# Hybrid S5 / gated DeltaNet / RWKV-7 block: triangular inverses from 16-blocks and masked products instead of 32-blocks

## The chip, the cores and the metric

One core of a Trainium2 chip runs the whole program in one launch. The metric is the device time of that core in microseconds, taken as the median of three runs. Engine names are those of the profile: PE is the matrix engine, PEld its weight loads, DVE the vector engine, ACT the scalar engine, POOL the general engine, and SP the engine whose queue issues every DMA of this kernel.

## What is computed

Two layers of a diffusion trunk. Each layer projects 256 context tokens and 512 latent tokens to three groups of heads, mixes them over the tokens, projects back and applies an MLP. Two of the three mixers work in chunks of 64 tokens, in both directions, and need per chunk, head and direction the inverse of a unit triangular 64 x 64 matrix. In the reference it stands as a solve:

```python
m = jnp.where(strict, jnp.einsum('bhnik,bhnjk->bhnij', kb, k) * decay, 0.0)
rhs = jnp.concatenate([v * beta[..., None], kb * jnp.exp(g)[..., None]], axis=-1)
sol = lax.linalg.triangular_solve(m + jnp.eye(C, dtype=m.dtype), rhs, left_side=True,
                                  lower=True, unit_diagonal=True)
...
def step(s, inp):
    kd_n, u_n, w_n, gl_n = inp[:4]
    v_new = u_n - jnp.einsum('bhck,bhkv->bhcv', w_n, s)
    s_next = s * jnp.exp(gl_n)[..., None, None] + jnp.einsum('bhck,bhcv->bhkv', kd_n, v_new)
```

The RWKV-7 mixer is a token-by-token scan in the reference; the kernel brings it to the same chunked form. The dense products (projections and MLP) are float32 with K = 1024 or 4096.

## The kernel before

The mixers' work is cut into 12 *pairs*, numbered 0 to 11 here: layer 0 context (pairs 0 to 2), layer 0 latents (3 to 5), layer 1 context (6 to 8), layer 1 latents (9 to 11). A pair holds one DeltaNet job and one RWKV job of two heads each. A context pair has 4 chunks, a latent pair 8. For a pair the kernel emits these steps:

- *prep* of both jobs (L1395 with `within`, L1359, and L1536): the strictly triangular matrices N. The last products of prep are L1622 and L1630 on PE; L1633 on POOL writes the last piece of N.
- *solve* (L335 to L386): the 32 x 32 diagonal blocks of N are stored to memory (L352), loaded so that every block lies on one partition (L363, L364), one half transposed by ACT (L366), inverted by substitution on DVE (L371, L373; 30 rounds of a product and a sum), transposed (L375), stored (L376 to L379) and loaded back into place (L352) together with transposes (L386).
- *prep2* (L1638): RWKV's b and k are transposed by PE (L481), copied by ACT (L1648) and parked in memory. It does not read the inverses. It frees the arena pages that held b and k.
- *post* (L1422, L1655): `level2` (L388) joins the 32-blocks to 64-blocks by two rounds of small products (L398, L404); then the inverses are applied (L1439, L1441, L1670 to L1682).
- *chain* (L1466, L1690): the recurrence over the chunks, on PE (L1488, L1502, L1511 for DeltaNet, L1708, L1722, L1732, L1733 for RWKV) and DVE (L1490, L1504, L1710, L1724) in turns.
- *readout*.

The order of emission is set by `run_jobs` (L1257): prep, solve and prep2 of pair i + 1 come ahead of post, chain and readout of pair i. Classes of priority (`CHAIN`, `LEVEL`, `READ`, `PREP`, `S5`, `DENSE`) let a scheduler take urgent work first, and it writes a fixed queue for each engine, which the engine works off in that order. Dense work (L296) and the S5 mixer (L779 to L900) are emitted in low classes and stand in the queues between the pairs' steps.

Two resources are handed out in the order of emission. PSUM banks come by tag with two buffers each: prep and prep2 use tag "p", post uses "q", the chains "gc" and "rc", dense work and S5 "d". SBUF comes from an arena of 18 pages (`s`, `scope`, `release`), so that a later tile can lie in a page that an earlier step still reads. The tile "solve" is a single buffer.

Of the kernel before, what the change touches and what calls it, by code (L numbers as in the profile page):

```python
# [12 lines left out]
OP = mybir.AluOpType  # L13
AX = mybir.AxisListType

P = 128
# [4 lines left out]
T = CT + LT  # L21
# [3 lines left out]
# tags of small shared tiles: columns, buffers  # L25
TAGS = {"s": (516, 6), "g1": (256, 3), "r1": (128, 3), "carry": (128, 6), "gup": (128, 2),
        "td": (24, 4), "tp": (24, 4), "tq": (24, 4), "tg": (24, 4), "tr": (24, 4), "t5": (8, 6), "wc": (24, 4),
        "solve": (2048, 1)}
# [12 lines left out]
for _n, _w in (("ident", 128), ("lt_f", 128), ("lt_b", 128), ("p_f", 128), ("p_b", 128),  # L41
               ("ones", 128), ("mr", 128), ("rm", 256), ("bo2", 2),
               ("sel2", 128), ("cent", 128), ("bo128", 128), ("scan", 512)):
    CONST[_n] = (_o, _w)
    _o += _w
# [19 lines left out]
class Part:  # L65
    """the context or the latents: first token, tokens, modulation's column."""
# [23 lines left out]
class Kern:  # L90
# [26 lines left out]
    def prio(self, c):  # L117
        """what is emitted inside is scheduled before the higher classes, in its own order."""
# [33 lines left out]
    def set_rounded(self, count):  # L152
        """makes count of the pages hold float32r."""
# [13 lines left out]
    def own(self, count, late, pieces):  # L167
        """lets what the pieces emit take its tiles from count pages of its own; late: jobs that they outlast."""
# [15 lines left out]
    def s(self, w, p=P, keep=None, kind=None):  # L184
# [12 lines left out]
                # early free, not beside tiles of another life, not across quarters and halves  # L197
# [36 lines left out]
    def load_layer(self, l):  # L234
# [4 lines left out]
        # derived columns  # L239
# [25 lines left out]
    def weight(self, src, eng):  # L265
        """the parts of 128 rows of up to 512 values; eng: the engines that take turns at the low one."""
# [9 lines left out]
    def rows(self, src, eng):  # L276
        """by row tile the parts of 4 x 128 rows of a block of 128 columns."""
# [12 lines left out]
    def product(self, ps, w, acts, first=True, last=True, fresh=False):  # L290
        """ps += sum over k of w[k].T @ act[k]; fresh: the low parts of acts come last."""
# [6 lines left out]
    def dense(self, src, acts, n, eng, fresh=False):  # L298
        """out^T[128 cols, tokens] for one block of 128 columns, in psum."""
# [6 lines left out]
    def rows_rstd(self, ps, n, scale, eps, tag):  # L306
        """(ps * scale + eps) ** -0.5 on a small token-major tile."""
# [7 lines left out]
    def bcast(self, r, w, sel, nt, tag, rt):  # L315
        """r [128 tokens, w per tile] back to feature-major, in psum; rt: scratch."""
# [18 lines left out]
    def solve(self, probs, nc_):  # L335
        """probs: pairs of blk, ytt. blk(h): [128, step, direction, 64] whose rows of half h hold strictly
        triangular blocks N on their diagonal; the inverses of I - N replace them. ytt takes the transposes
        of every first one."""
# [5 lines left out]

        def blocks(dram, store):
# [1574 lines left out]
```

## Time and profile before

| | |
|---|---|
| median of 3 runs | 3077.45 us (3076.12 to 3078.54) |
| span of the profiled execution, first to last instruction | 3056.7 us |
| PE / DVE / ACT / POOL busy | 87% / 60% / 39% / 37% of the span |
| granted PE clock, mean | 0.875 of 2.4 GHz |
| substitution on DVE (L371 and L373) | 720 instructions, 294.1 us |

The profile is of one execution; its own time is known as the span alone, and the runs' median is 20.75 us above it. A busy PE is not a PE at its peak, since records overlap and at half the clock the same work looks twice as long. Every float32 product leaves two records on PE.

### The profile page before, as it was taken

The page shows a single profiled execution, that of the slowest core. Times are in us where ns is not written, and L with a number is a line of the kernel's source. Part 1 is how long each engine was busy: PE and PEld are TensorE (multiplying, and loading weights), DVE is VectorE, ACT ScalarE, POOL GpSimd, SP SyncE. Part 2 cuts the span into 40 slices and gives each one's busy share as a digit, 9 for nine tenths or more (in the row PEclk, how much of TensorE's full clock was granted, in tenths as well). Part 3 has the DMA queues.
Part 4 walks back from the last instruction along what each step waited for, and adds up shares of the span by engine and source line. Part 5 has one row for each costly group of instructions (what it writes and reads, how often), then busy time and mean ns, then how long its engine had stood idle before and what let it go on. Part 6 is the DMA issues. An engine that isn't in the chain of part 4 may idle for free.

```text
span 3056.7 us, 54445 instructions
## 1 busy us (share of the span) xinstructions
PE 2669.4 (87%) x19956; PEld 2044.2 (67%) x19956; DVE 1833.7 (60%) x4462; ACT 1186.7 (39%) x2411; POOL 1134.5 (37%) x1274
## 2 busy tenths in 40 slices
PE   5789998865898999987899989889887889799998
PEld 1667776543566888876666768667655567477776
DVE  6654878765667756647876562647776753332223
ACT  2344445332534543445423423353334432133332
POOL 2532335424133121123446644344442522244443
PEclk9788999676787999987999999889987859699998
DMA  5345546543653543535233332255555632022222
GB/s 196 96 140 185 151 136 210 154 130 86 200 161 120 166 157 116 167 114 161 85 88 111 125 96 93 102 187 159 148 184 165 211 93 86 28 83 94 93 94 86
DMA packets 324651, 401.73 MB, mean 131 GB/s; under 512 B 142880, under 2 KB 173472, under 8 KB 324256
## 3 DMA queue, kind: packets, MB, share of 16 engines
q1 hardware_dynamic: 324384, 398.24, 41.6%
q8 instruction: 158, 2.59, 0.4%
q14 instruction: 109, 0.89, 0.1%
HBM read 300.76 MB, written 88.90 MB: 127 GB/s over the span
## 4 chain that ended last, share of the span: by engine, by line
PE 53%; DVE 19%; DMA 9%; issue 5%; ACT 4%; SPq 3%; POOL 1%; DVEq 0%; ACTq 0%; POOLq 0%
PE d L296 35%; DMA page<-dr 3%; DVE solve L371 3%; DVE solve L373 3%; PE rc L1733 2%; DVE wo L273 2%; PE rc L1732 2%; PE p L1622 1%; DVE s L472 1%; DMA dr<-page 1%; SPq L352 1%; DMA s<-s 1%; DMA wl<-in_w_dram 1%; ACT wh L272 1%; PE p L481 1%
## 5 line engine op out<-in xcount | busy, mean ns | idle before, releaser
L296 PE MATMUL d<-page,wh 128*128 128x512 f32 (+1 forms) x5024 | 1424.8, 367 | 61.0 <-DVE page L1156 15.5
L296 PEld LDWEIGHTS d<-page,wh 128*128 128x128 f32 x5024 | 919.0, 196 | 234.5 <-DVE page L1156 18.0
L296 PE MATMUL d<-page,wo 128*128 128x512 f32 (+1 forms) x2512 | 915.2, 365 | 5.5 <-DVE wo L273 4.3
L272 ACT CAST wh<-wl 128x512 fp32r<-128x512 f32 (+1 forms) x750 | 457.1, 616 | 710.2 <-PE d L296 421.0
L273 POOL TENSOR_TENSOR wo<-wl,wh 128x512 fp32r<-128x512 f32 (+1 forms) x357 | 471.8, 1325 | 672.0 <-ACT wh L272 635.8
L296 PEld LDWEIGHTS d<-page,wo 128*128 128x128 f32 x2512 | 493.4, 196 | 80.6 <-DVE wo L273 5.8
L273 DVE TENSOR_TENSOR wo<-wl,wh 128x512 fp32r<-128x512 f32 (+1 forms) x393 | 296.1, 758 | 112.6 <-ACT wh L272 104.1
L1156 DVE SCALAR_TENSOR_TENSOR page<-d,mod,page 128x512 f32<-128x512 f32 (+1 forms) x192 | 124.8, 659 | 199.6 <-PE d L296 199.1
L371 DVE TENSOR_TENSOR solve<-solve 128x30 f32<-128x30 f32 (+4 forms) x360 | 151.3, 420 | 21.6 <-issue 12.0
L1147 DVE TENSOR_TENSOR s<-s 128x512 f32<-128x512 f32 (+1 forms) x96 | 60.5, 631 | 172.1 <-ACT s L1146 172.0
L373 DVE TENSOR_TENSOR solve<-solve 128x30 f32<-128x30 f32 (+4 forms) x360 | 142.8, 397 | 7.7
L1499 POOL TENSOR_TENSOR g<-g,gates 64x128 f32<-64x128 f32 x120 | 59.5, 496 | 219.7 <-DVE g L1504 190.4
L285 DVE TENSOR_TENSOR page<-s,page 128x512 fp32r<-128x512 f32 (+1 forms) x118 | 86.6, 738 | 47.5 <-ACT page L284 47.3
L1146 ACT ACTIVATE s<-d 128x512 f32<-128x512 f32 (+1 forms) x96 | 50.6, 527 | 141.5 <-PE d L296 141.4
L472 DVE SCALAR_TENSOR_TENSOR s<-s,ncol,s 128x256 f32<-128x256 f32 (+1 forms) x132 | 96.4, 733 | 3.0
L284 ACT CAST page<-s 128x512 fp32r<-128x512 f32 (+1 forms) x118 | 64.1, 547 | 80.5 <-DVE s L1147 62.9
L926 PE MATMUL d<-wo,scp 128*2 128x512 f32 x160 | 76.3, 477 | 20.6 <-DVE wo L273 19.6
L1622 PE MATMUL p<-page,page 64*128 64x128 f32 (+1 forms) x576 | 84.7, 307 | 10.4 <-DVE page L1625 7.1
L1622 PEld LDWEIGHTS p<-page,page 64*128 64x128 f32 x576 | 73.1, 209 | 27.4 <-issue 12.8
L1733 PE MATMUL rc<-page,page 128*64 128x64 f32 x464 | 86.7, 275 | 2.8 <-DMA page<-dr 2.8
L481 PE MATMUL p<-consts,page 128*128 128x128 f32 x348 | 63.8, 309 | 25.0 <-DMA page<-dr 11.2
L1732 PE MATMUL rc<-page,r 64*64 64x64 f32 x432 | 79.2, 270 | 5.6 <-DVE r L1724 4.0
(464 smaller groups left out, 4057.7 us busy)
## 6 DMA issues: line engine op xcount, KB each, us to landing
wl<-in_w_dram SPq DMA_DIRECT2D x384, 256.0 KB, 2.6
wl<-in_mod_w_dram SPq DMA_DIRECT2D x160, 256.0 KB, 3.0
wl<-in_w_in_dram SPq DMA_DIRECT2D x142, 256.0 KB, 2.9
page<-dr SPq DMA_DIRECT2D x118, 256.0 KB, 3.3
dr<-s SPq DMA_DIRECT2D x72, 256.0 KB, 2.5
dr<-page SPq DMA_DIRECT2D x30, 512.0 KB, 4.1
dr<-page SPq DMA_DIRECT2D x55, 256.0 KB, 2.5
page<-dr SPq DMA_DIRECT2D x16, 834.0 KB, 5.2
```

The lines of the kernel that those rows point to most:

```text
L272: nc.scalar.copy(hi, st)
L273: low.tensor_tensor(lo, st, hi.bitcast(F32), OP.subtract)
L285: nc.vector.tensor_tensor(lo, src, hi.bitcast(F32), OP.subtract)
L296: nc.tensor.matmul(ps, x, y, start=(first and i == 0), stop=(last and i == len(order) - 1))
L371: nc.vector.tensor_tensor(tm, y3[:, :j, j:j + 1].to_broadcast([P, j, w]), y3[:, j:j + 1, j + 1:].to_broadcast([P, j, w]), OP.mult)
L373: nc.vector.tensor_tensor(y3[:, :j, j + 1:], y3[:, :j, j + 1:], tm, OP.add)
L472: nc.vector.scalar_tensor_tensor(acc, cp[:, j:j + n], w[:, 5 * i + j:5 * i + j + 1], acc, OP.mult, OP.add)
L481: self.nc.tensor.transpose(p[:, t * 128:(t + 1) * 128], src[:, t * 128:(t + 1) * 128], self.ident)
L1156: nc.vector.scalar_tensor_tensor(x[j], ps, mod[:, 40 + j, g:g + 1], x[j], OP.mult, OP.add)
L1622: nc.tensor.matmul(ps[:, i], flat(bk[d][hs, n0 + i]), kr[d][hs, n0 + i], start=True, stop=True)
L1732: nc.tensor.matmul(o, st[hs, d], kr[d][hs, n, 1], start=True, stop=False)
L1733: nc.tensor.matmul(o, xv[h][:, n, d], self.R[d][:, h, n], start=False, stop=True)
```

## The change

The substitution now inverts only the two 16 x 16 blocks on the diagonal of each 32-block, both in one instruction (`b2`, 14 rounds). A new step `level1` joins them to 32-blocks before the inverses go on: per job it makes two rounds of small products on PE in PSUM banks of tag "p", an ACT copy that scales by a 0/1 column (`lowhalf`), twelve DVE updates that read the products from PSUM under the same masks, and four POOL copies. The second load after the substitution now takes the transposes of both directions into the "solve" tile, which `level1` reads. Nothing else is moved in the source; all comments are removed, so line numbers from `solve` on shift (in `post` and `chain` by 39).

```diff
         "solve": (2048, 1)}
+        "solve": (2112, 1)}
...
+               ("ones", 128), ("mr", 128), ("rm", 256), ("bo2", 2), ("lowhalf", 2),
...
-        for j in range(30, 0, -1):
-            w = 31 - j
-            tm = yt[:, :j * w].rearrange("p (a b) -> p a b", a=j)
-            nc.vector.tensor_tensor(tm, y3[:, :j, j:j + 1].to_broadcast([P, j, w]),
-                                    y3[:, j:j + 1, j + 1:].to_broadcast([P, j, w]), OP.mult)
-            nc.vector.tensor_tensor(y3[:, :j, j + 1:], y3[:, :j, j + 1:], tm, OP.add)
+        b2 = w[:, :1056].rearrange("p (s x) -> p s x", s=2)[:, :, :512].rearrange("p s (a b) -> p s a b", b=32)
+        for j in range(14, 0, -1):
+            v = 15 - j
+            tm = yt[:, :2 * j * v].rearrange("p (s a b) -> p s a b", s=2, a=j)
+            nc.vector.tensor_tensor(tm, b2[:, :, :j, j:j + 1].to_broadcast([P, 2, j, v]),
+                                    b2[:, :, j:j + 1, j + 1:16].to_broadcast([P, 2, j, v]), OP.mult)
+            nc.vector.tensor_tensor(b2[:, :, :j, j + 1:16], b2[:, :, :j, j + 1:16], tm, OP.add)
...
-        blocks(dy, False)
-        dr = dt.rearrange("(j h k n d) a b -> j h k d a n b", j=len(probs), h=2, k=2, d=2)
-        for j, (_, ytt) in enumerate(probs):
-            for d in range(2):
-                for h in range(2):
-                    p0 = 64 * h + 32 * d
-                    nc.sync.dma_start(ytt[p0:p0 + 32], dr[j, h, d, d])
+        mts = [w[:, 512 * j:512 * j + 64 * nc_].rearrange("p (n d i) -> p n d i", d=2, i=32) for j in range(len(probs))]
+        for j, h, k, ps in places:
+            sb = probs[j][0][ps].rearrange("p n d i -> p (n d) i")[:, :, k * 32:k * 32 + 32]
+            nc.sync.dma_start(sb, split(dy)[j, h, k])
+            nc.sync.dma_start(mts[j][ps].rearrange("p n d i -> p (n d) i"), split(dt)[j, h, k])
+        for j, ((blk, ytt), mt) in enumerate(zip(probs, mts)):
+            self.level1(blk, mt, ytt, w[:, 1056 + 512 * j:1056 + 512 * j + 64 * nc_], nc_, "p")
+
+    def level1(self, blk, mt, ytt, qv, nc_, tag):
...
+        pv = blocks(self.ps(tag, n2), 32)
+        for n, d, p0 in every:
+            u, v = pair(slice(p0, p0 + 16), n, d, p0)
+            nc.tensor.matmul(pv[p0:p0 + 32, n, d], u, v, start=True, stop=True)
+        nc.scalar.mul(qv, pv.rearrange("p n d i -> p (n d i)"), hi)
+        qv = blocks(qv, 32)
+        po = self.ps(tag, 48 * nc_)
...
+        for n, d, p0 in every:
+            r = slice(p0, p0 + 32)
+            u, q = pair(r, n, d, p0)[0], qv[r, n, d]
+            outs = [(px[r, n, d], d == 0)] + [(pt[r, n], d == 1)] * (p0 % 64 == 32 * d)
+            for out, first in outs:
+                if first:
+                    nc.tensor.matmul(out, q, u[:, 16:], start=True, stop=True)
+                else:
+                    nc.tensor.matmul(out, u, q[:, :16], start=True, stop=True)
+        cut = ((16, hi), (0, lo))
+        for p0 in range(0, P, 32):
+            r = slice(p0, p0 + 32)
+            for d, (c, keep) in enumerate(cut):
+                x = blk[r, :, d, p0 % 64 + c:p0 % 64 + c + 16]
+                nc.vector.scalar_tensor_tensor(x, x, keep[r], px[r, :, d], OP.mult, OP.add)
...
+            nc.vector.scalar_tensor_tensor(ytt[r, :, c:c + 16], mt[r, :, d, c:c + 16], keep[r], pt[r], OP.mult, OP.add)
+            nc.gpsimd.tensor_scalar(ytt[r, :, 16 - c:32 - c], mt[r, :, d, 16 - c:32 - c], 1.0, None, OP.mult)
```

The order of the queues changes with it. The first place is PE's queue where prep of pair 11 ends and chain 10 is under way, in the kernel before. The names are: `p_` for banks of prep and prep2, `gc_` for the DeltaNet chain, `q_` for post. L1630 is the last product of prep 11, L481 is prep2 of pair 11, L1502 and L1511 are steps of chain 10, and L398 begins `level2` of pair 10.

```order
L1630 MATMUL p_24625<-page_117,page_4007 64x64
L481 MATMUL p_24745<-consts,page_109 128x128 x4
L481 MATMUL p_24751<-consts,page_109 128x128 x4
L481 MATMUL p_24759<-consts,page_115 128x128 x4
L481 MATMUL p_24765<-consts,page_115 128x128 x4
L1502 MATMUL gc_25096<-g_4050_25093,page_105 64x64 x2
L1502 MATMUL gc_25096<-g_4050_25093,page_97 64x64 x2
L481 MATMUL q_24905<-consts,page_119 128x128 x4
L481 MATMUL q_24915<-consts,page_4013 128x128 x4
L1511 MATMUL gc_25096<-page_115,g_4050_25093 64x64
L398 MATMUL q_24924<-page_97,page_111 32x32 x32
```

The same place in the changed kernel (L1669 is the former L1630, L1541 the former L1502, L403 the first round of `level1`):

```order
L1669 MATMUL p_27251<-page_117,page_4173 64x64
L1541 MATMUL gc_28048<-g_4098_28045,page_105 64x64 x2
L1541 MATMUL gc_28048<-g_4098_28045,page_97 64x64 x2
L403 MATMUL p_27339<-solve_27282,page_105 32x32 x4
L403 MATMUL p_27339<-page_105,solve_27282 32x32 x4
```

From there 320 products of `level1` (L403, L414, L416) stand in one piece, with nothing of another step between them, and behind the last of them (L520 is the former L481, L1550 the former L1511, L438 the former L398):

```order
L414 MATMUL p_27584<-solve_27282 32x16
L416 MATMUL p_27584<-solve_27282 32x16 x2
L414 MATMUL p_27584<-solve_27282 32x16
L520 MATMUL p_27697<-consts,page_109 128x128 x4
L520 MATMUL p_27703<-consts,page_109 128x128 x4
L520 MATMUL p_27711<-consts,page_115 128x128 x4
L520 MATMUL p_27717<-consts,page_115 128x128 x4
L520 MATMUL q_27857<-consts,page_119 128x128 x4
L520 MATMUL q_27867<-consts,page_4179 128x128 x4
L1550 MATMUL gc_28048<-page_115,g_4098_28045 64x64
L438 MATMUL q_27876<-page_97,page_111 32x32 x32
```

So prep2 of pair 11 and the rest of chain 10 have moved behind `level1` of pair 11.

The second place is PE's queue at the start of chain 9, in the kernel before. L481 here is prep2 of pair 10, which reads page_19841; L1488 is the first product of chain 9, which reads its W from the same page; L925, L926 and L839 are modulation and S5.

```order
L1630 MATMUL p_23519<-page_4009,page_97 64x64
L481 MATMUL p_23639<-consts,page_19841 128x128 x4
L926 MATMUL d_22019<-wo_22056,scp 2x512
L925 MATMUL d_22019<-wh_22063,scp 4x512
L926 MATMUL d_22019<-wo_22064,scp 2x512
L925 MATMUL d_22019<-wh_22071,scp 4x512
L926 MATMUL d_22019<-wo_22072,scp 2x512
L925 MATMUL d_22019<-wh_22079,scp 4x512
L839 MATMUL d_22096<-page_109,page_117 128x96
L481 MATMUL p_23645<-consts,page_19841 128x128 x4
L1488 MATMUL gc_23990<-g_3956_23987,page_19841 64x64 x2
L1441 MATMUL q_23767<-page_4009,page_111 64x64 x16
```

The same place in the changed kernel (L416 and L414 end `level1` of pair 10, L520 is prep2 of pair 10, L1527 the former L1488, L1480 the former L1441):

```order
L416 MATMUL p_26152<-solve_25850 32x16 x2
L414 MATMUL p_26152<-solve_25850 32x16
L520 MATMUL p_26265<-consts,page_21815 128x128 x4
L971 MATMUL d_24323<-consts,s_24321 128x4 x4
L964 MATMUL d_24330<-wh_24332,scp 4x512
L965 MATMUL d_24330<-wo_24333,scp 2x512
L964 MATMUL d_24330<-wh_24340,scp 4x512
L965 MATMUL d_24330<-wo_24341,scp 2x512
L964 MATMUL d_24330<-wh_24348,scp 4x512
L965 MATMUL d_24330<-wo_24349,scp 2x512
L1527 MATMUL gc_26616<-g_4000_26613,page_21815 64x64 x2
L1480 MATMUL q_26393<-page_4175,page_111 64x64 x16
```

Here the first product of chain 9 has moved from behind prep of pair 10 to behind `level1` and prep2 of pair 10.

## Rows read from the trace of the kernel before

**Rows 1.** The page, parts 1 and 2: engines' busy time; clock by slices.
```profile
PE 2669.4 (87%) x19956; PEld 2044.2 (67%) x19956; DVE 1833.7 (60%) x4462; ACT 1186.7 (39%) x2411; POOL 1134.5 (37%) x1274
...
PEclk9788999676787999987999999889987859699998
```

**Rows 2.** The page, part 4: the chain that ended last.
```profile
PE 53%; DVE 19%; DMA 9%; issue 5%; ACT 4%; SPq 3%; POOL 1%; DVEq 0%; ACTq 0%; POOLq 0%
PE d L296 35%; DMA page<-dr 3%; DVE solve L371 3%; DVE solve L373 3%; PE rc L1733 2%; DVE wo L273 2%; PE rc L1732 2%; PE p L1622 1%; DVE s L472 1%; DMA dr<-page 1%; SPq L352 1%; DMA s<-s 1%; DMA wl<-in_w_dram 1%; ACT wh L272 1%; PE p L481 1%
```

**Rows 3.** The page, part 5: the substitution's two groups.
```profile
L371 DVE TENSOR_TENSOR solve<-solve 128x30 f32<-128x30 f32 (+4 forms) x360 | 151.3, 420 | 21.6 <-issue 12.0
...
L373 DVE TENSOR_TENSOR solve<-solve 128x30 f32<-128x30 f32 (+4 forms) x360 | 142.8, 397 | 7.7
```

**Rows 4.** Busy time, clock and DMA of stretches of the mixers.
```profile
470.00:600.00 130.00, 110.39 (x998) 75.12 (x996) 110.15 (x317) 53.09 (x114) 64.91 (x74) 0.78 0.56 174
600.00:800.00 200.00, 139.46 (x1212) 94.51 (x1212) 116.59 (x321) 68.97 (x144) 60.44 (x64) 0.68 0.45 134
...
1000.00:1280.00 280.00, 267.29 (x2998) 236.87 (x2999) 192.90 (x547) 125.03 (x263) 42.95 (x61) 0.96 0.48 153
...
2000.00:2190.00 190.00, 167.13 (x1341) 126.64 (x1341) 127.25 (x294) 78.84 (x155) 85.75 (x101) 0.91 0.56 173
...
2400.00:2515.00 115.00, 93.95 (x1073) 68.14 (x1071) 72.57 (x183) 41.94 (x84) 44.27 (x47) 0.66 0.51 153
```

**Rows 5.** Instructions in order of time, around solve 11 (start, us, engine, line).
```profile
2450.41 1.49 POOL L1633 TENSOR_SCALAR page<-page 64x512 f32<-64x512 f32 x1 [8.58 <-PE p L1630]
...
2451.56 3.17 PE L481 MATMUL p<-consts,page 128*128 128x128 f32 x12 [0.25 <-ACT page L1632]
2451.92 0.85 SPq L352 DMA_DIRECT2D dr<-page  x2
...
2454.65 0.69 PE L1502 MATMUL gc<-g,page 64*64 64x64 f32 x8
...
2457.66 0.75 PE L398 MATMUL q<-page,page 32*32 32x32 f32 x64
...
2463.32 0.20 DVE L371 TENSOR_TENSOR solve<-solve 128x30 f32<-128x30 f32 x1
...
2464.60 0.25 DVE L373 TENSOR_TENSOR solve<-solve 128x84 f32<-128x84 f32 x1
```

**Rows 6.** One line's instructions from 2400 to 2520: ns min/median/max, first and last start.
```profile
L373 DVE TENSOR_TENSOR solve<-solve x30: 190/366/498, 2463.6 to 2494.0; 128x30 f32<-128x30 f32 x2, 128x58 f32<-128x58 f32 x2, 128x84 f32<-128x84 f32 x2, 128x108 f32<-128x108 f32 x2
L386 SPq DMA_DIRECT2D page<-dr x8: 325/449/1009, 2498.0 to 2507.7; - x8
```

**Rows 7.** In order of time, the first product of post 11.
```profile
2509.92 1.08 PE L398 MATMUL q<-page,page 32*32 32x32 f32 x64
```

**Rows 8.** The DeltaNet recurrence's DVE step (L1490): chains 9, 10 and 11.
```profile
L1490 DVE TENSOR_TENSOR g<-page,gc x16: 272/286/292, 2297.6 to 2369.5; 64x128 f32<-64x128 f32 x16
L1490 DVE TENSOR_TENSOR g<-page,gc x16: 274/286/292, 2453.1 to 2506.1; 64x128 f32<-64x128 f32 x16
L1490 DVE TENSOR_TENSOR g<-page,gc x16: 270/286/292, 2533.9 to 2590.3; 64x128 f32<-64x128 f32 x16
```

**Rows 9.** Groups by shape: busy us, mean ns of one, idle before.
```profile
L371 DVE TENSOR_TENSOR solve<-solve 128x84 f32<-128x84 f32 x24 | 9.0, 374 | 0.6
L373 DVE TENSOR_TENSOR solve<-solve 128x84 f32<-128x84 f32 x24 | 6.1, 256 | 0.7
L1724 DVE SCALAR_TENSOR_TENSOR r<-rc,wc,r 128x64 f32<-128x64 f32 x120 | 28.4, 278 | 10.4 <-PE rc L1722 7.7 <-POOL g L1480 0.8 <-PE gc L1511 0.6
L1442 ACT COPY page<-q 128x512 f32<-128x512 f32 x36 | 20.8, 586 | 13.6 <-PE q L1439 6.9 <-PE q L1441 4.7 <-PE p L481 0.9
```

**Rows 10.** PE's longest waits from 470 to 1000: total us, times, longest.
```profile
PE d L807 <- DMA page<-dr: 22.0, 4, 12.6
PE d L926 <- DVE wo L273: 12.3, 10, 5.3
PE d L885 <- DVE page L872: 11.1, 1, 11.1
```

**Rows 11.** In order of time, 64 x 64 products at the full clock.
```profile
2078.41 1.15 PE L1630 MATMUL p<-page,page 64*64 64x64 f32 x32
```

**Rows 12.** Prep 11: the DVE masks of its last products, columns as rows 6.
```profile
L1625 DVE TENSOR_TENSOR page<-p,consts x8: 406/412/424, 2429.5 to 2448.7; 128x256 f32<-128x256 f32 x8
```

More of the change, by code (lines that the diff above doesn't have):

```diff
@@ L343, in solve @@
         half = lambda t, d: t.rearrange("(x d) a b -> d x (a b)", d=2)[d]
-        def blocks(dram, store):
-            dr = dram.rearrange("(j h k x) a b -> j h k a x b", j=len(probs), h=2, k=2)
-            for j, (blk, _) in enumerate(probs):
-                for h in range(2):
-                    for k in range(2):
-                        p0 = 64 * h + 32 * k
-                        sb = blk(h)[p0:p0 + 32].rearrange("p n d i -> p (n d) i")[:, :, k * 32:k * 32 + 32]
-                        nc.sync.dma_start(*((dr[j, h, k], sb) if store else (sb, dr[j, h, k])))
-        dn = new("dn")
-        blocks(dn, True)
-        w = self.tile("solve", 2048)
-        y, yt = w[:, :1024], w[:, 1024:]
-        nc.gpsimd.memset(y, 0.0)
+        split = lambda dram: dram.rearrange("(j h k x) a b -> j h k a x b", j=len(probs), h=2, k=2)
+        places = [(j, h, k, slice(64 * h + 32 * k, 64 * h + 32 * k + 32))
+                  for j in range(len(probs)) for h in range(2) for k in range(2)]
+        dn = new("dn")
+        for j, h, k, ps in places:
+            sb = probs[j][0][ps].rearrange("p n d i -> p (n d) i")[:, :, k * 32:k * 32 + 32]
+            nc.sync.dma_start(split(dn)[j, h, k], sb)
+        w = self.tile("solve", 2080)
+        y, yt = w[:, :1024], w[:, 1056:2080]
+        nc.gpsimd.memset(w[:, :1056], 0.0)
         cube = lambda z: z.rearrange("p (a b) -> p a b", a=32)
         turned = lambda z: z.rearrange("p (a b) -> p b a", a=32)
-        y3 = cube(y)
         low, high = slice(0, m), slice(64, 64 + m)
@@ L379, in solve @@
         nc.sync.dma_start(half(dt, 1), y[high])
-        blocks(dy, False)
-        dr = dt.rearrange("(j h k n d) a b -> j h k d a n b", j=len(probs), h=2, k=2, d=2)
-        for j, (_, ytt) in enumerate(probs):
-            for d in range(2):
-                for h in range(2):
-                    p0 = 64 * h + 32 * d
-                    nc.sync.dma_start(ytt[p0:p0 + 32], dr[j, h, d, d])
+        mts = [w[:, 512 * j:512 * j + 64 * nc_].rearrange("p (n d i) -> p n d i", d=2, i=32) for j in range(len(probs))]
@@ new lines, in solve, with pair @@
+        for j, h, k, ps in places:
+            sb = probs[j][0][ps].rearrange("p n d i -> p (n d) i")[:, :, k * 32:k * 32 + 32]
+            nc.sync.dma_start(sb, split(dy)[j, h, k])
[3 more added lines that the diff above has]
+    def level1(self, blk, mt, ytt, qv, nc_, tag):
+        nc = self.nc
+        lo, hi = self.lowhalf[:, 0:1], self.lowhalf[:, 1:2]
+        diag = lambda p0: slice(p0 % 64, p0 % 64 + 32)
+        every = [(n, d, p0) for n in range(nc_) for d in range(2) for p0 in range(0, P, 32)]
+        n2 = 64 * nc_
+        blocks = lambda t, w: t.rearrange("p (n d i) -> p n d i", d=2, i=w)
+        def pair(r, n, d, p0):
+            x = blk[r, n, d, diag(p0)], mt[r, n, d]
+            return x if d == 0 else x[::-1]
+        pv = blocks(self.ps(tag, n2), 32)
[5 more added lines that the diff above has]
+        po = self.ps(tag, 48 * nc_)
+        px, pt = blocks(po[:, :32 * nc_], 16), po[:, 32 * nc_:].rearrange("p (n i) -> p n i", i=16)
+        for n, d, p0 in every:
[13 more added lines that the diff above has]
+                nc.vector.scalar_tensor_tensor(x, x, keep[r], px[r, :, d], OP.mult, OP.add)
+            d = p0 % 64 // 32
+            c, keep = cut[1 - d]
+            nc.vector.scalar_tensor_tensor(ytt[r, :, c:c + 16], mt[r, :, d, c:c + 16], keep[r], pt[r], OP.mult, OP.add)
+            nc.gpsimd.tensor_scalar(ytt[r, :, 16 - c:32 - c], mt[r, :, d, 16 - c:32 - c], 1.0, None, OP.mult)
@@ L397, in level2 @@
         for n, d, h in every:
-            nc.tensor.matmul(pq[b0(d, h), n], blk(h)[a0(d, h), n, d, cc(d)], ytt[a0(d, h), n], start=True, stop=True)
+            nc.tensor.matmul(pq[b0(d, h), n], blk[a0(d, h), n, d, cc(d)], ytt[a0(d, h), n], start=True, stop=True)
         with self.scope():
@@ L403, in level2 @@
             for n, d, h in every:
-                nc.tensor.matmul(py[a0(d, h), n], qs[b0(d, h), n], blk(h)[b0(d, h), n, d, cc(d)], start=True, stop=True)
+                nc.tensor.matmul(py[a0(d, h), n], qs[b0(d, h), n], blk[b0(d, h), n, d, cc(d)], start=True, stop=True)
             for d in range(2):
                 for h in range(2):
-                    nc.scalar.copy(blk(h)[a0(d, h), :, d, cc(d)], py[a0(d, h)])
+                    nc.scalar.copy(blk[a0(d, h), :, d, cc(d)], py[a0(d, h)])
     def gdn_gates(self, bgs, part, col):
@@ L1652, in problem @@
     def problem(self):
-        return lambda h: self.A, self.ytt
+        return self.A, self.ytt
     def post(self):
@@ L1658, in post @@
         nc = K.nc
-        K.level2(lambda h: A, self.ytt, part.nc, "q")
+        K.level2(A, self.ytt, part.nc, "q")
         xv = self.xv
```

9 lines of the change are left out of this document (4 added, 5 removed).

## The prediction

> **What bounds the kernel now.** I read the page first. PE is the busiest engine, 87% of the span, DVE the next with 60%, and the clock line falls to 0.5 and 0.6 in the slices where the mixers run: there PE is not full but waits for chains of small steps [rows 1]. The chain that ended last gives PE 53% and DVE 19%; the two lines of the substitution hold 3% each, no more than the dense products' helpers [rows 2]. The substitution is 720 instructions, 151.3 + 142.8 = 294.1 us of DVE, 24.5 us for each of the 12 pairs [rows 3]. A reader who stops here expects a gain.
>
> The stretches say where it could be had. From 1000 to 1280 PE is busy 267.29 of 280 us at clock 0.96: dense work fills every wait. From 470 to 600 it is 110.39 of 130, from 600 to 800 139.46 of 200, from 2400 to 2515 93.95 of 115 at clock 0.66, from 2000 to 2190 167.13 of 190: here waits are open [rows 4].
>
> Last I followed one solve, that of pair 11, where almost no dense work is left. Prep ends with POOL's copy at 2450.41 + 1.49 = 2451.90; the last stores leave at 2451.92, the first round of the substitution starts at 2463.32 (11.4 us later), the last at 2494.0, ending near 2494.2 (30.9 us), the transposed blocks are issued until 2507.7, and the first product that needs the inverses, L398, runs at 2509.92 (15.7 us) [rows 5 to 7]. The whole takes 58 us. What does PE do meanwhile? It runs chain 10: its DVE steps last from 2453.1 to 2506.1 [rows 8], so the solve of one pair lies beside the recurrence of the pair before. Chain 9 stands the same way beside solve 10, from 2297.6. The solve is long, but covered.
>
> **The change, part by part.**
>
> *Substitution.* In each solve 28 instructions of 28 to 112 values replace 60 of 30 to 240: 336 in all, 80 values on average. The nearest shape, 84 values, took 374 and 256 ns, 315 in the mean [rows 9]: 106 us instead of 294.
>
> *Twelve masked updates per job on DVE, 288 in all.* The nearest row that reads PSUM has 64 values, 278 ns [rows 9]: 80 us. So DVE loses 294 - 106 - 80 = 108 us of work.
>
> *Products.* A context job has 32 + 48, a latent job 64 + 96 (every block once, then once more, and half the blocks a second time for the transposes): 24 jobs make 2,880, two records each. 64 records of L398, also on 32-row blocks, took 0.75 us [rows 5], 11.7 ns a record: 67 us of PE. The other bound is that of L1630, 64-row blocks, 32 records in 1.15 us [rows 11]: 36 ns, 207 us. The new blocks are those of L398, so I take 67.
>
> The Trainium skill (TensorEngine Tiling, Instruction Overhead) says that each product carries some 60 cycles whatever its width. At 2.4 GHz that would be 25 ns a record and 144 us for the 5,760; the row of L398 does not bear this out for products that alternate between blocks (11.7 ns). By the page the sum below would be some 45 us higher.
>
> *Where the products stand.* This is the costly part. `level1` takes banks of tag "p", and so do prep2 and the next prep, which come later in emission. The order shows it: of pair 11, prep2 and the rest of chain 10 stand behind all 320 products, and chain 9's first product stands behind `level1` and prep2 of pair 10, whose page its W needs. PE works off its queue in order. So chain 10, which covered solve 11, now waits for it, and what waits behind PE there is DVE, POOL and ACT of the chain as well.
>
> The hold for one latent pair, by rows of pair 11: 11.4 us from prep's end to the first round as before; 28 instructions at some 0.28 us each, 8 us, if DVE is free (it is: the chain stands still), 14 at the old pace of 30.9 / 60 per instruction, so 9; 15.7 us as before to the landing; then `level1`, 640 records or 7.5 us, two ACT copies of 0.59 (L1442's row [rows 9]), the last job's updates 12 x 0.278 = 3.3, and a microsecond for hand-overs, 13 in all; prep2's transposes, 2451.56 + 3.17 with the first bank ahead of it, 4.5. Sum 53.6. In the kernel before chain 10 went on at 2454.65, 2.75 us after prep's end [rows 5]. The hold is 51 us; I use 50, with 40 and 65 as bounds.
>
> *Pairs 10 and 11: two holds, 100 us.* Against it, prep 11's first part now stands beside chain 9, where it came after; prep 11 lasted to 2448.7 and chain 9's DVE steps to 2369.5 [rows 8, 12], and I give back 20 of these 79 us (0 to 40). Net 80.
>
> *Earlier pairs.* Chains 0, 2 (its larger part), 3 and 8 stand behind the next solve in the same way; chains 4 and 6 too, with hundreds of dense products ahead. In the four stretches of rows 4 that are not full, PE idles 15%, 30%, 12% and 18% of the time, about a fifth: of 4 x 50 us, 40 are not filled (0 to 100).
>
> *Products elsewhere.* 15 of the 67 us lie in the two holds above; of the other 52 I count 30, since the rest falls into open waits.
>
> *DVE's relief.* 108 us less in its queue. The substitution's two lines hold 3% each of the chain that ended last, 6% of 3056.7 = 183 us [rows 2]; if the relief shortens that in proportion it is worth 183 x 108 / 294 = 67 us, the upper bound. Where the queue's next work waits for something else anyway it is worth nothing. I take 30. The solve's own start to finish no longer counts, since the hold contains it.
>
> *Order of S5.* With chains held, the queue takes S5's products earlier, ahead of pair 3 instead of beside it. There PE waited 22.0 us at L807 and 11.1 at L885 [rows 10]. I take 20 back (0 to 33).
>
> ACT's 24 copies (14 us in all) and POOL's 96 small ones lie in engines that are busy 39% and 37%; inside a hold they are counted. SP issues as many transfers as before.
>
> Sum: 80 + 40 + 30 - 30 - 20 = 100 us on the span of 3056.7: 3156.7, and with the 20.75 us by which the runs' median stands above the span, **3177 us**, 3.3% slower.
>
> **Rivals.**
>
> *Faster: the queue's order costs nothing.* If in a hold PE finds work (dense, S5, post), or the solve lands within 15 us of prep's end, chains lose nothing and the relief counts nearly whole: 3056.7 + 30 (products) - 60 (relief) - 20 (S5) + 20.75 = 3027 us. For it: DVE is on the chain for 19% [rows 2], and from 470 to 600, where solve 2 runs, it is busy 110.15 of 130 us [rows 4]. Against it: behind prep of pair 11 the queue holds only `level1`. It decides at one place: the gap on PE between prep 11's last product and the first of `level1`; under 15 us this rival holds.
>
> *No change.* Holds and gains cancel: 3077 us. For it: the holds of layer 0 are followed by 280 us of full dense work, into which lost time can be moved back; then 40 + 30 - 30 - 20 = 20 stays beside 80 of the end, so it needs 100 us of gains that I do not see.
>
> *Slower still: small products do not overlap.* If a record costs what L1630's does, 36 ns, the products take 207 us, 140 more; half of that on the path gives 3177 + 70 = 3247 us. For it: the second round writes 16 columns only and pairs of products share a block; the skill's 60 cycles point the same way. Against it: L398 at 11.7 ns.
>
> **How the numbers follow.** Forecast 0.56, still slower 0.20, faster 0.17, no change 0.07. Differences under 0.2% (6 us) can't be told from none here. Slower is 0.76, same 0.07, faster 0.17. The range begins where the forecast's terms stand at their low ends, holds of 40 us with 40 given back, none at the earlier pairs, relief of 67: 40 + 0 + 30 - 67 - 25 = -22, 3055 us. It ends at the third rival with holds of 65 us, 3247 + 30 = 3277, cut to 3265 since not all high ends come together. It leaves out the first rival and little of the third. For the forecast alone it is 3110 to 3230.
>
> **What would show it.** In the changed profile: between prep 11's end and chain 10's second step PE stands still for 45 to 60 us, ended by `level1`'s wait for the loads; DeltaNet's DVE steps of chain 10 begin once and go on only after it; from prep 10's end to the last chain's end it is some 80 us longer; the substitution falls to near 106 us of DVE and the updates to near 80; the 2,880 products take 60 to 80 us; and the slices of layer 1's latents have a lower clock. I am wrong if the queue's order lets chains start as before, if the solve lands in half of 50 us, or if dense work is so plentiful that early holds and the moved S5 work gain more than the end loses.

## The result and the profile after

The changed kernel takes 3298.7 us (median of 4 runs, 3296.32 to 3302.89) against 3076.78 of the kernel before in the same comparison: a ratio of 1.0741, interval 1.0708 to 1.0773. It is 222 us slower; 100 were forecast, and the time lies above the range. The profiled execution's span is 3294.5 us, 237.8 above that of before. In every run of this case whose span is known the time is 1.7 to 2.2 us above it, so of the 20.75 us between median and span before some 19 lie between two executions of the same kernel; the forecast of 100 us does not hang on them.

Of the page, engines' busy time and the clock by slices [rows 1]:

```profile
PE 2830.1 (86%) x25716; PEld 2165.0 (66%) x25716; DVE 1735.1 (53%) x4366; ACT 1201.2 (36%) x2435; POOL 1162.3 (35%) x1370
...
PEclk9879976676779999778899999888977667689999
```

PE is busy 160.7 us more and not busy 77.1 us more (3294.5 - 2830.1 = 464.4, where it was 387.3). It has 5,760 records more, as counted. DVE loses 98.6 us of work: it was 60% busy and is 53% busy now. The granted clock's mean falls from 0.875 to 0.841.

The new pieces, groups by line (L368 and L370 the substitution, L422 and L425 the updates, the others the products):

```profile
L368 DVE TENSOR_TENSOR solve<-solve 128x28 f32<-128x28 f32 (+6 forms) x168 | 46.7, 278 | 29.0 <-issue 26.3
L370 DVE TENSOR_TENSOR solve<-solve 128x28 f32<-128x28 f32 (+6 forms) x168 | 48.1, 286 | 3.4
L422 DVE SCALAR_TENSOR_TENSOR page<-page,consts,p 32x64 f32<-32x64 f32 (+1 forms) x192 | 52.0, 308 | 55.3 <-PE p L414 54.0
L425 DVE SCALAR_TENSOR_TENSOR page<-solve,consts,p 32x64 f32<-32x64 f32 (+1 forms) x96 | 29.3, 305 | 0.0
L403 PE MATMUL p<-solve,page 16*32 16x32 f32 x1152 | 42.6, 219 | 45.7 <-DMA solve<-dr 34.5 <-issue 9.6 <-DMA page<-dr 1.3
L414 PE MATMUL p<-page,solve 32*32 32x16 f32 x1152 | 42.4, 197 | 13.9 <-issue 9.6 <-ACT solve L404 4.3
```

The substitution takes 94.8 us of DVE (forecast 106), the updates 81.3 (forecast 80). A busy time of a product's group overlaps with the others'; with each moment of the trace given to the record that started first, all 5,760 records hold PE for 88 us (forecast 67). The same count is meant below where records *hold* PE.

The solve of pair 11, in order of time [rows 5 to 7]:

```profile
2657.24 1.49 POOL L1672 TENSOR_SCALAR page<-page 64x512 f32<-64x512 f32 x1 [1.88 <-PE p L1669]
...
2660.10 0.45 PE L1541 MATMUL gc<-g,page 64*64 64x64 f32 x8 [2.92 <-DVE g L1529]
...
2667.99 0.16 DVE L368 TENSOR_TENSOR solve<-solve 128x28 f32<-128x28 f32 x1 [6.80 <-issue]
...
2675.49 0.19 DVE L370 TENSOR_TENSOR solve<-solve 128x28 f32<-128x28 f32 x1
...
2684.20 0.70 PE L403 MATMUL p<-solve,page 16*32 16x32 f32 x4 [23.65 <-DMA solve<-dr]
...
2702.91 0.69 PE L520 MATMUL p<-consts,page 128*128 128x128 f32 x2
...
2710.47 0.45 PE L1550 MATMUL gc<-page,g 128*64 128x64 f32 x2
```

The hold stands there as forecast. Chain 10 takes a step that ends at 2660.55 and the next (L1550) at 2710.47, 49.9 us later; 51 was worked out. Its parts differ: 9.3 us to the first round (11.4 forecast), 7.7 for the substitution (9), 8.5 to the first product (15.7, since it waits for the first blocks only), 18.7 for `level1`'s products (13 with the updates), 7.6 for prep2 and on (4.5).

PE's waits, total us, times, longest:

```profile
PE p L403 <- DMA solve<-dr: 34.5, 17, 23.6
PE p L414 <- issue: 19.7, 8, 4.3
PE p L403 <- issue: 17.0, 8, 3.1
...
PE p L416 <- issue: 6.4, 5, 2.3
```

The first is the wait for the blocks. The other three, 43.1 us in 21 waits, are waits in which, by this view, no engine and no transfer was waited for. They stand in the middle of `level1`, and the prediction has no term for them.

Where the time went by pairs, from the first sum of each substitution, L373 before and L370 after (us; the last column is the end of the last chain's last DVE step):

| pair | 0 | 1 | 2 | 3 | 4 | 5 | 6 | 7 | 8 | 9 | 10 | 11 | end |
|---|---|---|---|---|---|---|---|---|---|---|---|---|---|
| before | 306 | 398 | 505 | 616 | 809 | 999 | 1434 | 1508 | 1775 | 2108 | 2304 | 2464 | 2623 |
| after | 309 | 446 | 603 | 735 | 909 | 1166 | 1584 | 1709 | 2004 | 2258 | 2472 | 2668 | 2862 |
| later by | 3 | 48 | 98 | 119 | 100 | 167 | 150 | 201 | 229 | 150 | 168 | 204 | 239 |

From pair 9 to the end 89 us are lost, where the prediction has 80. The other 150 are there at the solve of pair 6 and, after a rise to 229, at that of pair 9; the prediction has 20 for them (40 + 30 - 30 - 20).

### The profile page after: what moved, and what is told of

It is laid out like the page before. It is cut to its first block, busy times and chain, and to the rows that moved or that the text cites. A ratio compares the mean times of both kernels' runs of the same rounds, so it can differ in the third digit from the quotient of the medians.

```text
span 3294.5 us, 66216 instructions
## 1 busy us (share of the span) xinstructions
PE 2830.1 (86%) x25716; PEld 2165.0 (66%) x25716; DVE 1735.1 (53%) x4366; ACT 1201.2 (36%) x2435; POOL 1162.3 (35%) x1370
## 4 chain that ended last, share of the span: by engine, by line
PE 56%; DVE 13%; DMA 10%; issue 7%; ACT 4%; POOL 2%; SPq 2%; DVEq 0%; ACTq 0%; POOLq 0%
PE d L296 33%; PE p L1661 2%; DMA wl<-in_mod_w_dram 2%; DMA page<-dr 2%; PE rc L1772 2%; PE rc L1771 2%; DMA dr<-page 2%; DVE wo L273 2%; DVE s L511 1%; ACT wh L272 1%; DMA solve<-dr 1%; PE p L520 1%; DMA s<-s 1%; PE p L403 1%; DMA dr<-solve 1%
## 5 line engine op out<-in xcount | busy, mean ns | idle before, releaser
L426 POOL TENSOR_SCALAR page<-solve 32x64 f32<-32x64 f32 (+1 forms) x96 | 45.0, 469 | 164.1 <-DMA solve<-dr 160.3
L964 PE MATMUL d<-wh,scp 128*4 128x512 f32 x160 | 82.6, 517 | 21.8 <-ACT wh L272 18.0
L1771 PE MATMUL rc<-page,r 64*64 64x64 f32 x432 | 85.9, 290 | 6.6 <-DVE r L1763 3.3
L1749 DVE TENSOR_TENSOR page<-page,rc 64x128 f32<-64x128 f32 x144 | 40.9, 284 | 81.7 <-PE rc L1747 69.1
```

Source lines behind the costliest of these rows:

```text
L964: nc.tensor.matmul(ps[:4], self.scp[:, k], hi, start=(k == 0), stop=False)
L1771: nc.tensor.matmul(o, st[hs, d], kr[d][hs, n, 1], start=True, stop=False)
```

## Experiments

All ratios are to the kernel before, run in the same comparison (3061.7 to 3067.7 us there; 1% is 30.6 us).

**1. prep2 ahead of the solve.** This undoes the order alone: prep2 has its banks before `level1` takes them, and chains stand ahead of `level1` again.

```diff
+            step(PREP, at + 0.5, pair[1].prep2)
             step(PREP, at + 0.5, lambda: self.solve([j.problem() for j in pair], pair[0].part.nc))
-            step(PREP, at + 0.5, pair[1].prep2)
```

> The changed kernel with prep2 of a pair emitted ahead of its solve instead of behind it. The queue of PE then has chain i ahead of level1 of pair i + 1 at every pair, as in the kernel before; products, updates and rounds stay. Theory of the holds (the loss of 222 us comes from chains that stand behind level1 in PE's queue): most of it comes back, 3100 to 3170 us. Theory of the products (the 2,880 small products and the lower clock that they bring take the time, wherever they stand): within 30 us of the changed kernel, 3270 to 3310.

1.0432 (1.0386 to 1.0477). Between the two: 3.1 points, 95 us, come back, and 4.3 stay. Neither theory explains the loss alone.

**2. The same swap in the kernel before.**

> The kernel before with the same swap of prep2 and solve: a control. There prep2 does not wait for the solve, so both theories expect that it moves little: 3065 to 3090 us. If it is itself 50 us or more faster, what the swap brings in the changed kernel is not the end of a hold.

0.9924 (0.9902 to 0.9946): the swap is worth 23 us without any `level1`, which I did not expect. So of the 95 us some 72 are the end of a hold, if the two add up. Nothing is left out of this kernel's computation, and it is faster than both.

**3. The 14 rounds alone**, in place of the 30 (the loops over `j` in the diff above, without `level1`; the joins are left out of the computation).

> The kernel before with the substitution alone replaced by the 14 rounds on 16-blocks; nothing joins the 16-blocks, so the joins are left out of the computation. It tells the relief of DVE by itself. Prediction's term: 30 us, 3047 us, bounds 3010 to 3077. Theory that DVE's work was always covered: 3070 to 3080.

0.9857 (0.9804 to 0.9911): 44 us, inside the bounds of the prediction's term. That is what the 14 rounds bring by themselves.

**4. Wide products in place of the small ones, order as in the changed kernel.**

```diff
-        for n, d, p0 in every:
-            u, v = pair(slice(p0, p0 + 16), n, d, p0)
-            nc.tensor.matmul(pv[p0:p0 + 32, n, d], u, v, start=True, stop=True)
+        pb = self.ps(tag, n2)
+        nc.tensor.matmul(pb, self.ident, mt.rearrange("p n d i -> p (n d i)"), start=True, stop=True)
...
+        nc.tensor.matmul(po, self.ident, qv.rearrange("p n d i -> p (n d i)")[:, :48 * nc_], start=True, stop=True)
```

> The changed kernel in which each of the two rounds of small products of level1 is one 128-row product with the unit matrix into the same bank (48 of them in all, not 2,880); copies, updates, loads and the order of the queues stay. The joins are left out of the computation. Theory of the holds: the loss stays for its larger part, 3210 to 3280 us. Theory of the products: it goes, 3050 to 3130 us.

1.0452 (1.0405 to 1.0500). Most of the loss stays where the holds stay, and 2.9 points, 89 us, go with the small products, though the 48 wide ones hold PE for 44 us themselves. The time, 3201 us, lies just under the range of the theory of the holds.

**5 to 7. Both edits; then `level1` after the chain, with small and with wide products.**

```diff
-        for j, ((blk, ytt), mt) in enumerate(zip(probs, mts)):
-            self.level1(blk, mt, ytt, w[:, 1056 + 512 * j:1056 + 512 * j + 64 * nc_], nc_, "p")
+
+        def join():
+            for j, ((blk, ytt), mt) in enumerate(zip(probs, mts)):
+                self.level1(blk, mt, ytt, w[:, 1056 + 512 * j:1056 + 512 * j + 64 * nc_], nc_, "q")
+        self.join = join
...
         prepare(pairs[0], 0)
+        step(PREP, 0.5, self.join)
...
             step(READ, 4, r.readout)
+            if following and where != 3:
+                step(PREP, 1.7, self.join)
...
                 prepare(p, 1)
+                step(PREP, 1.5, self.join)
```

> The changed kernel with both edits of the first two experiments: prep2 ahead of the solve, and one wide product per bank in place of the small products (the joins are left out of the computation). If holds and products add up, each worth some 90 to 100 us, it stands 100 us below the two kernels with one edit, a ratio of 1.01 to 1.02 to the kernel before. If each of the two edits takes away the same wait (products are dear only because chains stand behind them), it stays within 30 us of them, a ratio above 1.035.

> The changed kernel with level1 of pair i + 1 emitted after the chain and readout of pair i and before prep of pair i + 2, in banks of tag q; products, updates and rounds stay. Neither the chain of the pair before nor prep of the next pair stands behind level1 in PE's queue (in the experiment with prep2 first, prep still did). Theory that prep is held too: 40 to 90 us below that experiment, a ratio of 1.015 to 1.03. Theory that what is left there is the products' own time on PE: within 15 us of it, 1.04 to 1.05.

> The same with one wide product per bank in place of the small products (the joins are left out of the computation). No hold and no small product are left; rounds, loads, copies and updates stay. Theory that holds and products make up the whole loss: near the kernel with 14 rounds alone, a ratio of 0.985 to 1.0. Theory that updates, copies and the longer road from the loads to the products cost as well: 1.005 to 1.02.

With both edits 1.0067 (1.0037 to 1.0097): they add up, to somewhat more than their sum. With wide products and no hold of prep either, 0.9966 (0.9943 to 0.9989): the hold of prep (with the change of tag) is worth one point. But with the small products the same order gives 1.0556 (1.0532 to 1.0581), worse than experiment 1, against both theories. There the small products cost 5.9 points, 181 us. The whole spans, the sixth kernel and then the seventh (span, then busy time and count of PE, PEld, DVE, ACT, POOL, then the clock):

```profile
0.00:3225.00 3225.00, 2846.39 (x25716) 2197.16 (x25716) 1737.10 (x4366) 1200.98 (x2435) 1156.65 (x1370) 0.84 0.41 126
```

```profile
0.00:3041.30 3041.30, 2687.40 (x20052) 2050.89 (x20052) 1743.44 (x4366) 1201.26 (x2435) 1176.82 (x1370) 0.89 0.43 133
```

PE stands still only 25 us longer (378.6 against 353.9) but is busy 159 us longer. The products hold 105.5 us instead of the 38.9 of the wide ones, 67 more; the other 92 belong to the 19,956 records that both kernels share, while the mean clock is 0.84 and not 0.89. A stretch of the sixth kernel shows it:

```profile
2480.00:2540.00 60.00, 58.47 (x830) 41.51 (x826) 23.76 (x73) 8.46 (x16) 16.16 (x20) 0.55 0.24 77
```

PE is busy 58.47 of 60 us there and granted little over half of its clock. Of the stretches of 60 us, taken every 10 us, in which PE is at least 95% busy, none has a mean clock under 0.73 in the kernel before and under 0.81 in the seventh.

The other two pairs of kernels with small and with wide products divide otherwise. The page's first lines for experiments 4, 1 and 5, whose spans are 3196.7, 3190.6 and 3071.7 us:

```profile
PE 2752.4 (86%) x20052; PEld 2080.4 (65%) x20052; DVE 1730.3 (54%) x4366; ACT 1201.5 (38%) x2435; POOL 1174.2 (37%) x1370
```

```profile
PE 2817.8 (88%) x25716; PEld 2172.3 (68%) x25716; DVE 1745.7 (55%) x4366; ACT 1200.1 (38%) x2435; POOL 1172.6 (37%) x1370
```

```profile
PE 2698.5 (88%) x20052; PEld 2058.9 (67%) x20052; DVE 1742.7 (57%) x4366; ACT 1200.9 (39%) x2435; POOL 1176.8 (38%) x1370
```

What small products cost more than wide ones, in us of one profiled execution each (executions of one kernel differ by 10 us and more):

| order | span | PE held by the products | PE's other records | PE stands still |
|---|---|---|---|---|
| as changed (4 to the change) | +98 | +44 | +34 | +20 |
| prep2 first (5 to 1) | +119 | +61 | +59 | 0 |
| after the chain (7 to 6) | +184 | +67 | +92 | +25 |

So in no order is the price mainly one of waiting; with prep2 first, where waits for nothing come to 5.0 us in all of `level1`, nothing of it is.

**8 and 9. Wide and small products**, in the order of the sixth kernel and in that of the changed one: the wide product of experiment 4 goes into each bank first, and the small ones write over it.

> The kernel with level1 after the chain (ratio 1.056) with the wide product added ahead of the small ones in each bank, which then overwrite it: all the small products and 48 wide ones, so PE has some 40 us more to do. Theory of the clock (small products keep PE occupied at half the clock, and it is the clock of everything beside them that costs): the wide products bring the clock back in these stretches, ratio 1.00 to 1.035 and a mean granted clock above 0.86. Theory of PE's own time (each product costs what it occupies): slower by the wide products, 1.060 to 1.080.

> The changed kernel itself with the same wide products added ahead of its small ones, order as in the changed kernel. Theory of the clock: 1.03 to 1.06 where the changed kernel stands at 1.074. Theory of PE's own time: 1.078 to 1.095.

1.0584 (1.0529 to 1.0640) and 1.0831 (1.0781 to 1.0881). The theory of the clock falls in the form in which I had put it: the mean clock stands at 0.852 and 0.842, where it was 0.844 and 0.841, and 48 wide products do not bring it back. The other theory holds in the ninth kernel, 0.9 points slower; the eighth is 0.3 points slower, less than it asked and within the noise. In the ninth the waits for nothing fall from 43.1 to 20.2 us, yet PE stands still as long as before, 465.2 us for 464.4.

**10. `level1` after the chain, in the class of the chains** (`step(CHAIN, 1.7, self.join)`).

> The kernel with level1 after the chain, with level1 in the class of the chains instead of that of prep, so that its products stand closer together in PE's queue (for pair 11 within 250 places, where 344 were). Theory that the join comes late because its products are strewn between the steps of two chains (there 76 us from the substitution's end to the last update of pair 11): 1.02 to 1.04. Theory that it costs the same wherever it stands: 1.045 to 1.065.

1.0452 (1.0404 to 1.0499), one point better than the sixth kernel and at the lower end of the second theory's range. The class is worth about 32 us there; most of the price stays.

**11 and 12. Small products issued twice**, in both rounds, in the changed kernel and in that of experiment 1.

```diff
-        for n, d, p0 in every:
+        for n, d, p0 in every * 2:
```

> The changed kernel with each round of small products issued twice into the same places: 5,760 products, 11,520 records, nothing else changed. Theory that the products cost their records at the pitch of the full clock (9 to 10 ns, 55 us for 5,760 records more): ratio 1.088 to 1.097. Theory that they cost records plus the lower clock of everything beside them, as the 89 to 112 us that their removal gave: 1.100 to 1.115.

> The same doubling in the kernel with prep2 ahead of the solve (ratio 1.043), where chains do not stand behind level1. Records at the full clock: 1.057 to 1.065. Records plus clock: 1.075 to 1.090.

1.1281 (1.1264 to 1.1298) and 1.1102 (1.1064 to 1.1140): 165 and 205 us for 5,760 records more, 29 and 36 ns each, above both theories. So it is not the full clock's pitch of the records alone. Of the profiled executions' 159 us in the eleventh kernel 85 are the products' hold of PE (15 ns for each record more) and 72 standing still; of 219 in the twelfth 91, 60, and 69 that PE's other records take longer. PE's waits in the eleventh kernel:

```profile
PE p L403 <- issue: 42.1, 25, 4.5
PE p L416 <- issue: 32.6, 19, 3.3
PE p L414 <- issue: 31.3, 18, 2.8
```

The waits for nothing have grown from 43.1 to 106.0 us. In order of time, one piece of it, PE's waits alone:

```profile
1006.05 0.18 PE L414 MATMUL p<-solve 32*32 32x16 f32 x1 [1.79 <-issue]
...
1010.19 0.26 PE L403 MATMUL p<-page,solve 16*32 16x32 f32 x2 [1.81 <-issue]
...
1013.93 0.31 PE L403 MATMUL p<-page,solve 16*32 16x32 f32 x3 [1.82 <-issue]
```

They come about every 4 us, after 126 to 128 records each, wherever in the loop that falls. The page's queue of instructions tells why: 158 loads before, 203 after, 248 with the products doubled. Every load in the trace has 16,384 bytes; 45 loads for 5,760 records are 128 bytes a record, so 128 records (64 products, with their weight loads) use up one load:

```profile
q8 instruction: 158, 2.59, 0.4%
```

```profile
q8 instruction: 203, 3.33, 0.4%
```

```profile
q8 instruction: 248, 4.06, 0.5%
```

Set beside the packets of this queue, all 21 waits of the changed kernel end 1.3 to 1.6 us after such a load has landed, and so do 61 of the 62 here, within 1.2 to 1.6. PE was waiting for its instructions.

**13. Small products by themselves**, at the end of the kernel before, where nothing else wants PE.

```diff
+            for k in range(512):
+                small(k)
+            for k in range(24):
+                large(k)
+            for g in range(8):
+                for k in range(64):
+                    small(k)
+                for k in range(6):
+                    large(k)
```

> The kernel before with extra products at its very end, whose results nobody reads: 512 small products of 32x32 blocks in one piece (1,024 records), 24 products of 128x512, then eight times 64 small ones and 6 of 128x512. Theory of the instruction feed (PE's instructions come in loads of 16 KB, one for 128 records of products, and PE stands still where it works through them faster than they come): in the first piece PE stops after every 128 records or so for 1.4 to 2.1 us with no engine to wait for, 26 to 34 ns a record in all, 27 to 35 us; in the mixed piece the stops are shorter or gone, as the large products give time for a load. Theory that stops come from the places of level1 in the queue: the 1,024 records run through at 9 to 14 ns, 10 to 15 us. Theory that the clock goes with it: the granted clock falls to half in the first piece, though PE had run dense work at full clock until a few microseconds before it, and comes back in the mixed piece.

In order of time, PE:

```profile
3076.59 3.30 PE L1259 MATMUL d<-consts 32*32 32x32 f32 x234
3081.90 1.30 PE L1259 MATMUL d<-consts 32*32 32x32 f32 x128 [2.01 <-issue]
3085.92 1.93 PE L1259 MATMUL d<-consts 32*32 32x32 f32 x128 [2.72 <-issue]
3089.93 1.93 PE L1259 MATMUL d<-consts 32*32 32x32 f32 x128 [2.09 <-issue]
3093.95 1.93 PE L1259 MATMUL d<-consts 32*32 32x32 f32 x128 [2.09 <-issue]
3097.43 1.93 PE L1259 MATMUL d<-consts 32*32 32x32 f32 x128 [1.54 <-issue]
3101.17 1.93 PE L1259 MATMUL d<-consts 32*32 32x32 f32 x128 [1.81 <-issue]
3104.91 0.54 PE L1259 MATMUL d<-consts 32*32 32x32 f32 x22 [1.82 <-issue]
3105.38 23.32 PE L1261 MATMUL d<-consts 128*128 128x512 f32 x48
3128.63 1.29 PE L1259 MATMUL d<-consts 32*32 32x32 f32 x128
```

And busy time of PE, clock and DMA in stretches (us, PE busy, clock, DMA share, GB/s):

```profile
3040.00:3060.00 20.00, 19.39 (x85) 1.00 0.23 69
...
3069.40:3076.50 7.10, 4.79 (x14) 0.50 0.00 0
3076.50:3079.60 3.10, 3.10 (x226) 0.50 0.44 157
3079.63:3083.00 3.37, 1.36 (x152) 1.00 0.96 357
3083.05:3085.90 2.85, 0.15 (x14) 0.50 0.40 144
3085.90:3105.40 19.50, 10.14 (x663) 0.50 0.02 4
...
3110.40:3128.60 18.20, 18.20 (x43) 1.00 0.00 0
3128.60:3181.20 52.60, 52.60 (x1121) 1.00 0.01 3
```

The theory of the feed holds. 234 records run without a stop; then PE stops after every 128 for 1.5 to 2.7 us, each time until 1.2 to 1.6 us after a load has landed. It goes on every 3.5 to 4.0 us, and the 1,024 records take 28.9 us, 28 ns each, of which only 10 (at the full clock, 1.29 / 128) to 15 (at half, 1.93 / 128) are work. With six large products after each 64 small ones the stops are gone, 128 records take 1.29 us and the clock stays at 1.00.

The part on the clock holds only in part. The clock was at half before the first small product ran, from 3069.4 us on, after the dense work had ended at 3067.1. It stood at 1.00 from 3079.6 to 3083.0, after small products had run for 3 us without a stop, and at half again after the first stop, while PE was busy 10.14 of 19.50 us. It came back in the 24 large products, ahead of the mixed piece.

## Why the prediction was wrong

In points of the ratio, by kernels that differ in one step each (every step is uncertain by 0.4 to 0.6 points, 12 to 18 us):

| from | to | points | us |
|---|---|---|---|
| before | 14 rounds alone | -1.4 | -44 |
| 14 rounds | `level1` without small products, nothing held | +1.1 | +33 |
| | next prep held too (experiment 7 to 5) | +1.0 | +31 |
| | chains held too (5 to 4) | +3.9 | +118 |
| | small products for wide (4 to the change) | +2.9 | +89 |

The third step also moves `level1` to another tag, and the fourth contains the 23 us of experiment 2, which have nothing to do with `level1`. The last step depends on the order: the same exchange is 112 us from experiment 5 to 1, and 181 from 7 to 6.

**Substitution, updates, relief of DVE: right.** 94.8, 81.3 and 44 us, forecast 106, 80 and 30. That the solve is long but covered held: a kernel that spends 163 us less of DVE (1670.4 for 1833.7) and joins nothing gains 44.

**The hold: right in mechanism, place and size.** 49.9 us at chain 10, and 118 us in all less 23 of the swap, where 80 and 40 were forecast. That the single hold fits to a microsecond is partly luck: its parts were forecast 10.6 us too long up to the first product and 8.8 too short behind it. PE itself was to stand still there for 45 to 60 us and does so for 23.6, then it works on `level1`. The rival in which the queue's order costs nothing was to be told by the gap between the last product of prep 11 and the first of `level1`: it is 27 us, and 15 was the point.

**Order of S5: about right by its waits.** L807's wait, 22.0 us, is 12.2 (L846 now), and L885's, 11.1, is under 5.3: 16 us or more of waits are gone, 20 were forecast. No run shows what this is worth by itself.

**"Products elsewhere": the step that failed.** It took 52 us of the products outside the two holds and counted 30; what replacing them gives is 89, against wide products that are not free themselves. Three things stand in place of the 30. The pitch was taken from a row at clock 1.00, 64 records of L398 in 0.75 us [rows 5]; the same 64 took 1.08 us, 16.9 ns each, at clock 0.50 [rows 7], and the products of `level1` hold PE for 88 us, 15.3 ns a record and not 11.7. PE's busy time and clock before, while the one and while the other row ran:

```profile
2457.70:2458.40 0.70, 0.70 (x66) 1.00 0.98 205
2509.90:2511.00 1.10, 1.10 (x66) 0.50 0.00 0
```

PE's other records take 34 us longer beside them than beside wide products. And PE waits 43.1 us for its instructions, though it stands still for only 20 us more than with wide products. L398 shows 64 records, and a load of instructions holds 128: the row could not show what a run of 640 does. The third rival had a dear record with the right size, 36 ns (28 to 36 all in, experiments 11 to 13), but for another reason, that records would not overlap. They do.

The Trainium skill (TensorEngine Tiling (Array Packing), Instruction Overhead) puts some 60 cycles on each matmul; at 2.4 GHz that is 25 ns by estimate. The row of the mixed piece, 128 records in 1.29 us, does not bear this out: it is 10 ns a record and 20 ns a product of two records. The prediction set the 25 ns against a record; set against a product, they are near the 23 ns that L398's row gives. That the starved records took 28 ns has another reason, the loads.

**Terms that were missing.** `level1` stands ahead of the next pair's prep too, in the same banks (31 us). The prediction names the next prep among what takes these banks behind `level1`, follows only the chain of the pair before, and gives the prep no time. And `level1` with nothing held and wide products costs 33 us more than the 14 rounds alone; these products hold PE for 39 us, and what copies, updates and the longer road to the inverses cost beside them is not separated. With the 59 us by which "products elsewhere" fell short these two make 123 us, and the forecast lacked 122; what the other terms were off nearly cancels. How the 150 us of the earlier pairs divide among the steps no run shows.

**The clock.** The records that both kernels share take 2830.1 - 88 = 2742 us after and 2669.4 before: 73 us more for the same records. By the profiled executions 51 of them come where the chains are held (experiment 5 to 4) and 34 with the small products (4 to the change); the other steps give back 12. So part of the price of a hold is the slower work around it. The forecast named slices of a lower clock and gave them no time.

What stays open is why the clock is lower. In the thirteenth kernel starved small products stood at half the clock, and unstarved ones came to run at the full one. But in the sixth kernel, where waits for instructions come to 3.5 us and PE is full, it is down as well, and wide products did not bring it back. Nor was it settled why the small products cost 181 us in the order of the sixth kernel and 112 in that of the first; 34 of the 65 us more of span lie in PE's other records and 25 in standing still.

## What to carry to other kernels

Count the instructions that a step puts into one queue in one piece: where small products are worked through faster than their loads come (here 128 records, 64 float32 products, a load), the engine waits for the next load, which a row of 64 records does not show. Take the pitch of small products from a row at the clock that their place will have. When a step takes banks of a tag, list all that takes the same tag behind it, the next round's work as well as this round's. An engine's time that is saved behind other work is worth only what the rest of the chain gives back (44 us here, for 163 of DVE); a kernel with the saving alone, and nothing of what pays for it, measures that bound first.

## What the runs showed of the hardware

PE's instructions came in loads of 16,384 bytes, one per 128 float32 products' records (64 products), at one load per 3.5 to 4.0 us when PE was starved: 28 ns a record. PE went on 1.2 to 1.6 us after a load had landed. Small products in alternating 32-row blocks ran at 10 ns a record at 2.4 GHz and 15 at 1.2 GHz, less than twice as slow. In a stretch of such products in which PE was busy 52% of the time it was granted 1.2 GHz; 234 of them in one piece, 3.3 us, began at 1.2 GHz and ended at 2.4. Small products between the steps of recurrences, with PE busy 97% of 60 us, were granted 0.55 of 2.4 GHz in the mean.
